# Differential attention: a score block as one product of 128 rows in place of two

## The chip, the cores and the metric

The kernel runs on one core of a Trainium2 chip. Time is device time in microseconds (us) from the start to the end of one execution of the program. Four engines work side by side and meet at semaphores: PE (TensorE, the matrix products), DVE (VectorE), ACT (ScalarE) and POOL (GpSimd, hardly used here); SP issues the DMA transfers. Each engine has its own list of instructions, whose order is fixed when the program is built. The tiles of this kernel have 128 partitions (rows) by up to 512 columns; a product contracts over the rows of both its operands.

## The reference, cut to what matters

Two layers of a decoder trunk, 512 tokens, width 1024. Each layer is a half-step SwiGLU feed-forward block, a mixer of four groups of heads (A differential attention, B causal convolution, C gated MLP, D forgetting attention), and a second feed-forward block. The change is in group A:

```python
z = hn @ w_in[l]
qa = _rms_norm(z[..., DIFF_Q0:DIFF_K0].reshape(B, S, DIFF_HEADS, 2, DIFF_QK_DIM), diff_qk_g[l, 0])
ka = _rms_norm(z[..., DIFF_K0:DIFF_V0].reshape(B, S, DIFF_HEADS, 2, DIFF_QK_DIM), diff_qk_g[l, 1])
...
s = jnp.einsum('bqhcd,bkhcd->bhcqk', qi, k).astype(jnp.float32) * scale
causal = k_pos[None, :] <= q_pos[:, None]
p = jax.nn.softmax(jnp.where(causal, s, NEG_INF), axis=-1)
a = p[:, :, 0] - lam * p[:, :, 1]
return jnp.einsum('bhqk,bkhe->bqhe', a.astype(v.dtype), v)
```

There are 4 heads, each with two score maps (c = 0, 1) of 32 channels. Queries go in blocks of 128, so block i needs (i + 1) · 128 keys.

## The kernel before, in words

**Precision.** A value that goes into a projection or a score is kept as a high part, rounded to the operand type fp32r, and a low part, the remainder. Each projection product is three PE products: high by high, low by high, high by low (`mm3`, lines L337 to L339). Weights arrive by DMA; ACT rounds each 512-column piece to the high part `wh` (L288) and DVE subtracts to get the low part `wl` (L289).

**The mixer's order.** The input projection goes by groups: b, aqk (Q and K of group A), av, dqk, dvf (Q, K, V and gates of group D), c, then the output projection wo. While these products are written out, the work of the groups that already have their inputs is mixed in by Python generators (`chain_a` to `chain_d`): a virtual clock counts up with each product, after each projection product a `tick` lets those generators go on that are due by it, and each of them names its next due time when it yields (`GA`, two units of that clock, between steps of group A). A list scheduler then fixes each engine's order; the two instructions of `softmax` on DVE and ACT are given a higher priority. What stands between two pieces of attention on PE are projection products (called fillers below), and they are what PE does while DVE and ACT work on the attention.

**Group A.** There are 16 units per layer, unit u = 4 · head + query block. A step of `attention_gen` writes out the weighting by V of the unit two before (`poA`), `stage1_a` of this unit, and the transposes of the unit before (`ptA` on PE, copied by ACT to `pT`, L1026). `stage1_a` forms the two score blocks `scA`: in `scores` two products of 128 rows each and one bf16 product of `maskb` by `identb` that adds the mask; DVE takes the negated row maximum `nmA` (L1007), ACT the exponential (L1009). DVE then takes the reciprocal `rA`, the factor `cf` (L1184) and the combination `p` of the two maps (L1185). `ptA` waits for that `p`.

**Preparation of a head.** `prep_a(hd, 0)` makes the Q operands and `prep_a(hd, 1)` the K operands of a head; those of head hd + 1 are written out in units 1 and 2 of head hd. Four PE transposes bring `zr`, in which each 32-channel group stands twice, into PSUM (`aT`). For Q, ACT makes the high part `aTh` (L1207) and, for each map, a scaled copy `aTx` (L1212), and DVE makes of both a tile `aTs` for each map (L1214): its own 64 rows hold [high; low], the other 64 rows are zero. For K, ACT makes `aTh` and DVE the remainder `aTs` (L1219). A score block is then the Q tile by the high K tile plus the Q tile by the low K tile. Among DVE's other work are the taps of group B's convolution (`cacc`, L1130) and the scaling of group D's Q and K (`dqk`, L1279).

Of the kernel before, what the change touches and what calls it, by code (L numbers as in the profile page):

```python
# [9 lines left out]
F32 = mybir.dt.float32  # L10
F32R = mybir.dt.float32r
BF16 = mybir.dt.bfloat16
I32 = mybir.dt.int32
AF = mybir.ActivationFunctionType
ALU = mybir.AluOpType
AX = mybir.AxisListType

P = 128
# [6 lines left out]
def tile_hybrid_trunk(  # L25
# [29 lines left out]
    V, A, G, T = nc.vector, nc.scalar, nc.gpsimd, nc.tensor  # L55
# [27 lines left out]
    const = ctx.enter_context(tc.tile_pool(name="const", bufs=1))  # L83
# [4 lines left out]
    small = ctx.enter_context(tc.tile_pool(name="small", bufs=2))  # L88
# [3 lines left out]
    def blk(dt=F32, name="blk"):  # L92
        return bpool.tile([P, 512], dt, tag="blk", name=name)
# [4 lines left out]
    def att(name="at"):  # L98
        return pat.tile([P, 512], F32, tag="at", name=name)
# [38 lines left out]
    def matmul(out, fp32=True, **kw):  # L138
        n = 1
        for d in out.shape[1:]:  # L140
            n *= d
        clock[0] += max(0.107, n * (4 if fp32 else 1) / 2400.0)
        return T.matmul(out, **kw)  # L143

    def transpose(**kw):
        clock[0] += 0.107
        return T.transpose(**kw)
# [12 lines left out]
    onesc = const.tile([P, P], F32, name="onesc")  # L160
    V.memset(onesc, 1.0 / 256.0)


    slot = const.tile([P, 2, 2], F32, name="slot")
    V.memset(slot, 0.0)
    for r in range(4):
        V.memset(slot[32 * r : 32 * r + 32, r // 2, 0:1], 1.0 - 2.0 * (r % 2))
        V.memset(slot[32 * r : 32 * r + 32, r // 2, 1:2], float(r % 2))
    fold = const.tile([P, P], F32, name="fold")
    V.tensor_reduce(fold[:, :32], ident.rearrange("p (g c) -> p c g", g=4), AX.X, ALU.add)  # L170
    for g in range(1, 4):
# [244 lines left out]
    for i in range(NT // 2):  # L416
        r = wpool.tile([P, 2048], F32, tag="wl", name=f"x{i}")
# [255 lines left out]
    r = rsqrt(ss0, NT, 1.0 / D, "n000", 0, False)  # L673
# [133 lines left out]
    for q in range(1, 4):  # L807
# [8 lines left out]
        ps = att(f"adaps0{q}")  # L816
# [187 lines left out]
    def softmax(sc, n, ssum, name):  # L1004
        nm = small.tile([P, 1], F32, tag="nm", name=f"nm{name}", bufs=8)
        with tc.high_priority(offset=HX):
            V.tensor_reduce(nm, sc[:, :n], AX.X, ALU.max, negate=True)  # L1007
            p = blk(name="p")
            A.activation(p[:, :n], sc[:, :n], AF.Exp, bias=nm, accum_out=ssum)  # L1009
        return p  # L1010

    def scores(pairs, i, name, fp32=True):
        n = (i + 1) * P
        sc = att(f"sc{name}")
        for e, (q, k) in enumerate(pairs):
            matmul(sc[:, :n], fp32=fp32, lhsT=q[:, i * P : (i + 1) * P], rhs=k[:, :n], start=e == 0, stop=False,
                   skip_group_check=True)
        matmul(sc[:, i * P : n], fp32=False, lhsT=identb, rhs=maskb, start=False, stop=True, skip_group_check=True)
        return sc
# [51 lines left out]
    def mixer(l, hn, before, nxt):  # L1071
# [14 lines left out]
        V.tensor_scalar(nlam, nlam, -lam_init, None, ALU.add)  # L1086
        ogs = small.tile([P, 1], F32, tag="ogs", name=f"ogs{l}")
        V.tensor_scalar(ogs, cols[:, col_at["og"] + l : col_at["og"] + l + 1], 1.0 - lam_init, None, ALU.mult)
        gA = small.tile([P, 4], F32, tag="gA", name=f"gA{l}")
        a0 = col_at["aq"] + 2 * l  # L1090
        V.tensor_scalar(gA[:, 0:1], cols[:, a0 : a0 + 1], 32 ** -0.5, None, ALU.mult)
        V.tensor_copy(gA[:, 1:2], cols[:, a0 + 1 : a0 + 2])
        V.tensor_scalar(gA[:, 2:4], slot[:, :, 1], gA[:, 0:1], None, ALU.mult)
        gD = small.tile([P, 2], F32, tag="gD", name=f"gD{l}")
        V.memset(gD, 1.0)
        d0 = col_at["dq"] + 2 * l
# [74 lines left out]
        aT = {}  # L1171

        def stage1_a(i, hd):
            n = (i + 1) * P
            s = small.tile([P, 2], F32, tag="sA", name=f"sA{l}{i}{hd}", bufs=4)
            r = small.tile([P, 2], F32, tag="rA", name=f"rA{l}{i}{hd}", bufs=6)
            pp = []
            for cc in range(2):
                q, (kh, kl) = aT[hd][0][cc], aT[hd][1]
                sc = scores(((q, kh), (q, kl)), i, f"A{l}{i}{hd}{cc}", False)  # L1180
                pp.append(softmax(sc, n, s[:, cc : cc + 1], f"A{l}{i}{hd}{cc}"))
            V.reciprocal(r, s)
            cf = small.tile([P, 1], F32, tag="cf", name=f"cf{l}{i}{hd}", bufs=4)
            V.scalar_tensor_tensor(cf, s[:, 0:1], nlam, r[:, 1:2], ALU.mult, ALU.mult)  # L1184
            V.scalar_tensor_tensor(pp[0][:, :n], pp[1][:, :n], cf, pp[0][:, :n], ALU.mult, ALU.add)  # L1185
            if hd < H - 1 and i in (1, 2):
                prep_a(hd + 1, i - 1)
            return pp[0], r[:, 0:1]
# [11 lines left out]
        def prep_a(hd, w):  # L1200


            ps = att(f"aT{l}{hd}{w}")
            for t in range(NT):
                transpose(out=ps[:, t * P : (t + 1) * P], in_=zr[t, w][:, hd * P : (hd + 1) * P], identity=ident)
            hi = blk(F32R, "aTh")
            A.activation(hi, ps, AF.Identity, scale=gA[:, w : w + 1])  # L1207
            if w == 0:
                sts = []
                for cc in range(2):  # L1210
                    x_low = blk(name="aTx")
                    A.activation(x_low, ps, AF.Identity, scale=gA[:, 2 + cc : 3 + cc])  # L1212
                    st = blk(F32R, "aTs")
                    V.scalar_tensor_tensor(st, hi.bitcast(F32), slot[:, cc, 0:1], x_low, ALU.mult, ALU.add)  # L1214
                    sts.append(st)
                aT[hd] = [sts]
            else:
                st = blk(F32R, "aTs")
                V.scalar_tensor_tensor(st, ps, gA[:, 1:2], hi.bitcast(F32), ALU.mult, ALU.subtract)  # L1219
                aT[hd].append((hi, st))  # L1220

        def chain_a():
            rsa = rsqrt(ssa, 64, 1.0 / 32.0, f"a{l}", RSA)
# [192 lines left out]
    for l in range(L):  # L1416
        gen = start(ada_gen(36 * l + 36 if l == 0 else 36 * (l + 1)), delay=1.0 if l == 0 else AD)
        hn2 = {}
        before = ffn(l, 0, hn, before, (l, 1, hn2))
        finish(gen)  # L1420
        hn3 = {}
        before = mixer(l, hn2, before, (l, 2, hn3))
        gen = start(ada_gen(36 * (l + 1) + 32), delay=AD)
        hn = {}
        before = ffn(l, 2, hn3, before, (l + 1, 0, hn) if l + 1 < L else None)
        finish(gen)
# [30 lines left out]
```

## Time and profile before

| what | value |
| --- | --- |
| median of 3 runs | 1978.57 us (1978.0 to 1978.98) |
| the profiled execution: its own time | 1977.61 us |
| its span from the first to the last instruction | 1975.7 us |
| mean granted TensorE clock in it, as a share of 2.4 GHz | 0.995 |
| PE busy | 1953.3 us, 99% of the span |
| DVE busy | 1228.0 us, 62% |
| ACT busy | 725.0 us, 37% |

A share of the span is a mean over stages that differ. The mixer of the first layer lies at about 445 to 615 us, that of the second about 970 us later. "Busy" of PE counts an instruction until its result is out, so products that overlap count once; what one product costs in a row of products is the distance from its start to the next start (called its pitch below).

### The profile page before, as it was taken

The numbers are of one execution on the slowest core, as the hardware profiler recorded it, in microseconds if no ns is written. First come the engines' busy times: TensorE is split into PE (matmuls) and PEld (weight loads), VectorE is DVE, ScalarE is ACT, GpSimd is POOL, SyncE is SP. The second block draws the span as 40 slices with busy tenths as digits, with TensorE's granted clock in tenths as the row PEclk, the third lists the DMA queues.
The fourth block names the chain that finished last, engine by engine and source line by source line (L and its number), as shares of the span: only waits on it lengthen the run. The fifth ranks groups of instructions, "written<-read, shape, count | busy, mean of one in ns | idle before, by whom it ended". The sixth has DMA issues, their size and how long they took to land.

```text
span 1975.7 us, 26197 instructions
## 1 busy us (share of the span) xinstructions
PE 1953.3 (99%) x10296; PEld 1661.3 (84%) x10296; DVE 1228.0 (62%) x2608; ACT 725.0 (37%) x1512; POOL 5.6 (0%) x18
## 2 busy tenths in 40 slices
PE   9999999999999999999999999999999999999999
PEld 7888888997889888888898888889787898888888
DVE  7776675688977776677585333347887773333332
ACT  5323223435764323222342222234377642222230
POOL 0000000000000000000000000000000000000000
PEclk9999999999999999999999999999999999999999
DMA  9675665221212466566334332322212122332311
GB/s 306 195 251 193 212 206 177 92 77 52 70 52 76 163 222 213 197 208 211 130 129 128 107 107 89 103 95 82 86 43 70 43 78 81 119 100 93 107 64 43
DMA packets 165350, 250.54 MB, mean 127 GB/s; under 512 B 6292, under 2 KB 112236, under 8 KB 165228
## 3 DMA queue, kind: packets, MB, share of 16 engines
q1 hardware_dynamic: 164640, 247.73, 38.0%
q8 instruction: 80, 1.31, 0.3%
q0 software_dynamic: 352, 1.05, 0.2%
q14 instruction: 42, 0.34, 0.1%
q10 hardware_dynamic: 236, 0.10, 0.0%
HBM read 246.76 MB, written 2.10 MB: 126 GB/s over the span
## 4 chain that ended last, share of the span: by engine, by line
PE 91%; DVE 6%; DMA 1%; issue 1%; ACT 1%; SPq 0%; DVEq 0%
PE i L337 15%; PE i L338 15%; PE i L339 15%; PE o L337 8%; PE o L338 8%; PE o L339 8%; DVE cacc L1130 1%; PE wo L337 1%; PE wo L339 1%; PE wo L338 1%; PE ia L781 1%; DMA ada<-in_ada_w_dram 1%; DVE wl L289 1%; PE scA L143 1%; PE scD L143 1%
## 5 line engine op out<-in xcount | busy, mean ns | idle before, releaser
L289 DVE TENSOR_TENSOR wl<-w,wh 128x512 fp32r<-128x512 f32 (+3 forms) x652 | 401.3, 663 | 318.8 <-ACT wh L288 318.3
L288 ACT CAST wh<-w 128x512 fp32r<-128x512 f32 (+3 forms) x652 | 352.4, 600 | 663.8 <-issue 384.2
L337 PE MATMUL i<-hnh,wh 128*128 128x512 f32 (+1 forms) x1408 | 526.5, 376 | 2.2 <-ACT hnh L630 2.2
L338 PE MATMUL i<-hnl,wh 128*128 128x512 f32 (+1 forms) x1408 | 527.2, 375 | 0.3
L339 PE MATMUL i<-hnh,wl 128*128 128x512 f32 (+1 forms) x1408 | 526.4, 375 | 0.0
L337 PEld LDWEIGHTS i<-hnh,wh 128*128 128x128 f32 x1408 | 264.1, 188 | 49.8 <-ACT hnh L630 2.6
L338 PEld LDWEIGHTS i<-hnl,wh 128*128 128x128 f32 x1408 | 264.8, 188 | 48.0 <-DVE hnl L623 0.7
L339 PEld LDWEIGHTS i<-hnh,wl 128*128 128x128 f32 x1408 | 264.7, 188 | 47.5
L337 PE MATMUL o<-acth,wh 128*128 128x512 f32 (+1 forms) x832 | 297.9, 358 | 0.2 <-DVE h L868 0.2
L338 PE MATMUL o<-actl,wh 128*128 128x512 f32 (+1 forms) x832 | 296.8, 357 | 0.0
L339 PE MATMUL o<-acth,wl 128*128 128x512 f32 (+1 forms) x832 | 296.6, 356 | 0.0
L337 PEld LDWEIGHTS o<-acth,wh 128*128 128x128 f32 x832 | 157.2, 189 | 23.1 <-DVE h L868 0.6
L339 PEld LDWEIGHTS o<-acth,wl 128*128 128x128 f32 x832 | 157.2, 189 | 22.5
L338 PEld LDWEIGHTS o<-actl,wh 128*128 128x128 f32 x832 | 157.2, 189 | 22.5
L501 DVE SCALAR_TENSOR_TENSOR acc<-ada,cond,acc 128x512 f32<-128x512 f32 x224 | 154.5, 745 | 26.6 <-DMA ada<-in_ada_w_dram 26.4
L937 DVE TENSOR_TENSOR silu<-silu,i 128x512 f32<-128x512 f32 x82 | 56.3, 687 | 158.8 <-PE i L339 158.7
L939 ACT CAST acth<-silu 128x512 fp32r<-128x512 f32 x88 | 54.4, 618 | 223.4 <-DVE silu L937 223.4
L868 DVE SCALAR_TENSOR_TENSOR h<-o,modc,h 128x512 f32<-128x512 f32 (+1 forms) x112 | 73.9, 671 | 70.5 <-PE o L339 69.9
L1130 DVE SCALAR_TENSOR_TENSOR cacc<-yp,cwc,cacc 128x512 f32<-128x512 f32 x120 | 89.5, 746 | 1.4
L941 DVE TENSOR_TENSOR actl<-silu,acth 128x512 fp32r<-128x512 f32 x88 | 60.6, 688 | 27.4 <-ACT acth L939 27.4
L630 ACT ACTIVATE hnh<-hn,modc 128x256 fp32r<-128x256 f32 x80 | 38.9, 506 | 71.8 <-DVE hn L629 71.8
L934 ACT ACTIVATE silu<-i 128x512 f32<-128x512 f32 x82 | 48.8, 596 | 31.9 <-PE i L339 31.9
(336 smaller groups left out, 2363.1 us busy)
## 6 DMA issues: line engine op xcount, KB each, us to landing
w<-in_ffn_w_in_dram SPq DMA_DIRECT2D x166, 512.0 KB
ada<-in_ada_w_dram SPq DMA_DIRECT2D x64, 1024.0 KB
w<-in_ffn_w_out_dram SPq DMA_DIRECT2D x40, 1024.0 KB
w<-in_w_in_dram SPq DMA_DIRECT2D x18, 1024.0 KB
w<-in_w_out_dram SPq DMA_DIRECT2D x8, 1024.0 KB
w<-in_ffn_w_in_dram SPq DMA_DIRECT2D x18, 256.0 KB
fpb<-in_ada_w_dram SPq DMA_DIRECT2D x16, 256.0 KB
w<-in_ffn_w_out_dram SPq DMA_DIRECT2D x8, 512.0 KB
```

What stands on the lines that cost most here:

```text
L288: A.copy(wh[:, a], r[:, a])
L289: V.tensor_tensor(wl[:, a], r[:, a], wh[:, a].bitcast(F32), ALU.subtract)
L337: T.matmul(ps, lhsT=lh, rhs=rh, start=start, stop=False)
L338: T.matmul(ps, lhsT=lh, rhs=rl, start=False, stop=False)
L339: last_t[0] = T.matmul(ps, lhsT=ll, rhs=rh, start=False, stop=stop)
L501: last_v[0] = V.scalar_tensor_tensor(acc, src, cond[:, k : k + 1], acc, ALU.mult, ALU.add)
L868: V.scalar_tensor_tensor(h[m][:, a:b], ps[:, a:b], mcol(l, j, m), h[m][:, a:b], ALU.mult, ALU.add)
L934: A.activation(gates[j], ps, AF.Silu)
L937: last_v[0] = V.tensor_tensor(s, s, ps, ALU.mult)
L939: A.copy(ah, s)
L941: V.tensor_tensor(al, s, ah.bitcast(F32), ALU.subtract)
L1130: V.scalar_tensor_tensor(acc, ysl, w, acc, ALU.mult, ALU.add)
```

## The change

In a score block, the two products with a Q tile that is half zeros become one. The Q tile of a map now holds [high; low] in its own 64 rows and a copy of the same in the other 64; the K tile of a map holds the high part in the own 64 rows and the low part in the other 64. One product over 128 rows then sums high by high, low by high, high by low and low by low.

```diff
-    slot = const.tile([P, 2, 2], F32, name="slot")
-    V.memset(slot, 0.0)
+    slot = const.tile([P, 2], F32, name="slot")
     for r in range(4):
-        V.memset(slot[32 * r : 32 * r + 32, r // 2, 0:1], 1.0 - 2.0 * (r % 2))
-        V.memset(slot[32 * r : 32 * r + 32, r // 2, 1:2], float(r % 2))
+        V.memset(slot[32 * r : 32 * r + 32, 0:1], 1.0 - 2.0 * (r % 2))
+        V.memset(slot[32 * r : 32 * r + 32, 1:2], float(r % 2))
...
-        V.tensor_scalar(gA[:, 2:4], slot[:, :, 1], gA[:, 0:1], None, ALU.mult)
+        V.tensor_tensor(gA[:, 2:3], slot[:, 1:2], gA[:, 0:1], ALU.mult)
...
-                q, (kh, kl) = aT[hd][0][cc], aT[hd][1]
-                sc = scores(((q, kh), (q, kl)), i, f"A{l}{i}{hd}{cc}", False)
+                sc = scores(((aT[hd][0][cc], aT[hd][1][cc]),), i, f"A{l}{i}{hd}{cc}", False)
...
-            hi = blk(F32R, "aTh")
-            A.activation(hi, ps, AF.Identity, scale=gA[:, w : w + 1])
+            own = (slice(0, 64), slice(64, 128))
+            st = [blk(F32R, "aTs") for _ in range(2)]
             if w == 0:
-                sts = []
+                hi = blk(F32R, "aTh")
+                A.activation(hi, ps, AF.Identity, scale=gA[:, 0:1])
+                x_low = blk(name="aTx")
+                A.activation(x_low, ps, AF.Identity, scale=gA[:, 2:3])
                 for cc in range(2):
-                    x_low = blk(name="aTx")
-                    A.activation(x_low, ps, AF.Identity, scale=gA[:, 2 + cc : 3 + cc])
-                    st = blk(F32R, "aTs")
-                    V.scalar_tensor_tensor(st, hi.bitcast(F32), slot[:, cc, 0:1], x_low, ALU.mult, ALU.add)
-                    sts.append(st)
-                aT[hd] = [sts]
+                    a, b = own[cc], own[1 - cc]
+                    V.scalar_tensor_tensor(st[cc][a], hi[a].bitcast(F32), slot[a, 0:1], x_low[a], ALU.mult, ALU.add)
+                    A.copy(st[cc][b], st[cc][a].bitcast(F32))
+                aT[hd] = [st]
             else:
-                st = blk(F32R, "aTs")
-                V.scalar_tensor_tensor(st, ps, gA[:, 1:2], hi.bitcast(F32), ALU.mult, ALU.subtract)
-                aT[hd].append((hi, st))
+                for cc in range(2):
+                    a, b = own[cc], own[1 - cc]
+                    A.activation(st[cc][a], ps[a], AF.Identity, scale=gA[a, 1:2])
+                    V.scalar_tensor_tensor(st[cc][b], ps[a], gA[a, 1:2], st[cc][a].bitcast(F32), ALU.mult, ALU.subtract)
+                aT[hd].append(st)
```

The change also moves instructions, since the virtual clock counts the products that are gone and the scheduler places the new ones. Counted over the projection products of dqk, dvf and c (96 of dqk, then 96 of dvf, then c), so many stand on PE ahead of a unit's first score product in each layer, before and after the change: unit 3: 36 and 53; unit 6: 67 and 89; unit 8: 95 and 139; unit 9: 113 and 157; unit 10: 163 and 192; unit 11: 185 and 192; unit 12: 192 and 192; unit 15: 224 and 224.

PE's order, first layer, around unit 11 (head 2, block 3, scores of 512 columns). Before, from the mask product of its second score block to the first scores of unit 12 (`scA_4647`); `ptA_4596` belongs to unit 10 and `poA_4640` to the weighting of unit 10:

```order
L143 MATMUL scA_4584<-maskb,identb 128x128
L339 MATMUL dvf_3_4396<-wh_4153,hnl 128x260
L337 MATMUL dvf_3_4396<-wh_4153,hnh 128x260
L338 MATMUL dvf_3_4396<-wl_4154,hnh 128x260
L339 MATMUL dvf_3_4396<-wh_4153,hnl 128x260
L147 MATMUL ptA_4596<-ident,p 128x128 x3
L337 MATMUL dvf_3_4396<-wh_4153,hnh 128x260
L338 MATMUL dvf_3_4396<-wl_4154,hnh 128x260
L339 MATMUL dvf_3_4396<-wh_4153,hnl 128x260
L143 MATMUL poA_4640<-va,pT 128x64 x3
L143 MATMUL scA_4647<-aTh,aTs 128x128
```

After, the same engine from the transposes that prepare head 3's K (`aT_4513`), behind the scores of unit 10, to the first scores of unit 12 (`scA_4630`); `ptA_4524` and `poA_4555` are unit 9's, `ptA_4579` and `poA_4623` unit 10's, `scA_4561` and `scA_4568` the two score blocks of unit 11:

```order
L147 MATMUL aT_4513<-ident,zr 128x128 x4
L147 MATMUL ptA_4524<-ident,p 128x128 x2
L143 MATMUL poA_4555<-va,pT 128x64 x2
L143 MATMUL scA_4561<-aTs 128x512
L143 LDWEIGHTS identb
L143 MATMUL scA_4561<-maskb,identb 128x128
L143 MATMUL scA_4568<-aTs 128x512
L143 LDWEIGHTS identb
L143 MATMUL scA_4568<-maskb,identb 128x128
L147 MATMUL ptA_4579<-ident,p 128x128 x3
L143 MATMUL poA_4623<-va,pT 128x64 x3
L143 MATMUL scA_4630<-aTs 128x128
```

The fillers have moved ahead of unit 9 and unit 10: in this piece none is left, where before 22 stood between unit 9's transposes and its weighting, 4 ahead of unit 10's transposes and 3 ahead of its weighting. All 192 of dqk and dvf stand ahead of it, and c begins behind the transposes of unit 11 in both.

DVE's order at the same place, first layer, from the combination of unit 10 to that of unit 11. Before (`cf_4527` is unit 10's, `nmA_4580` and `nmA_4588` are unit 11's maxima):

```order
L1185 SCALAR_TENSOR_TENSOR p<-p,cf_4527 128x384
L1007 TENSOR_REDUCE nmA_4580<-scA_4576 128x1
L1007 TENSOR_REDUCE nmA_4588<-scA_4584 128x1
L289 TENSOR_TENSOR wl_4607<-w_4407,wh_4606 128x512 x2
L1182 RECIPROCAL rA_4575<-sA_4574 128x2
L289 TENSOR_TENSOR wl_4607<-w_4407,wh_4606 128x512
L1184 SCALAR_TENSOR_TENSOR cf_4593<-sA_4574,nlam_3260,rA_4575 128x1
L1130 SCALAR_TENSOR_TENSOR cacc<-yp_3567,cwc,cacc 128x512
L1185 SCALAR_TENSOR_TENSOR p<-p,cf_4593 128x512
```

After (`cf_4510` is unit 10's, `nmA_4564` and `nmA_4571` are unit 11's maxima, `nmA_4633` is the first of unit 12):

```order
L1182 SCALAR_TENSOR_TENSOR p<-p,cf_4510 128x384
L1219 SCALAR_TENSOR_TENSOR aTs<-aT_4513,gA_3264,aTs 64x512
L287 TENSOR_TENSOR wl_4590<-w_4394,wh_4589 128x512
L1005 TENSOR_REDUCE nmA_4564<-scA_4561 128x1
L1005 TENSOR_REDUCE nmA_4571<-scA_4568 128x1
L287 TENSOR_TENSOR wl_4590<-w_4394,wh_4589 128x512
L1128 SCALAR_TENSOR_TENSOR cacc<-yp_3566,cwc,cacc 128x512
L1179 RECIPROCAL rA_4560<-sA_4559 128x2
L287 TENSOR_TENSOR wl_4730<-w_4599,wh_4729 128x512
L1181 SCALAR_TENSOR_TENSOR cf_4576<-sA_4559,nlam_3259,rA_4560 128x1
L1005 TENSOR_REDUCE nmA_4633<-scA_4630 128x1
L1182 SCALAR_TENSOR_TENSOR p<-p,cf_4576 128x512
```

From unit 10's first maximum to unit 11's combination, DVE now has one `aTs`, two `wl` and one maximum more (that of unit 12); ahead of unit 10's first maximum it has three `aTs` more and one `wl` less. On ACT, after the change, one cast of the first wo chunk and then the two exponentials of unit 10, half of head 3's K, three more casts of that chunk and the other half of K stand in this order ahead of unit 9's `pT`; both exponentials of unit 11 stand ahead of unit 10's `pT`, as before, but unit 12's scores are now built on PE behind the weighting that needs that `pT` with no filler between. The second layer has the same order in all of this.

## Rows read from the trace of the kernel before

**Rows 1.** The page, section 1: busy time, share of the span, instructions.

```profile
PE 1953.3 (99%) x10296; PEld 1661.3 (84%) x10296; DVE 1228.0 (62%) x2608; ACT 725.0 (37%) x1512; POOL 5.6 (0%) x18
```

**Rows 2.** Waits of PE, whole run: us in total, times, longest us.

```profile
PE poA L143 <- ACT pT L1026: 1.8, 2, 0.9
PE ptA L147 <- DVE p L1185: 1.4, 2, 0.7
```

**Rows 3.** Windows: us, then PE, PEld, DVE, ACT, POOL busy, PEclk, DMA, GB/s.

```profile
490.00:500.00 10.00, 10.00 (x81) 9.50 (x80) 9.98 (x28) 8.02 (x23) 0.00 (x0) 1.00 0.04 8
...
510.00:520.00 10.00, 8.43 (x58) 7.06 (x56) 9.58 (x27) 8.28 (x28) 0.50 (x1) 1.00 0.39 133
```

**Rows 4.** Timeline of PE, units 10 to 13: start, us, instruction, [idle before].

```profile
503.51 0.42 PE L143 MATMUL scA<-aTh,aTs 128*128 128x384 f32 x1
503.77 0.34 PE L143 MATMUL scA<-aTs 128*128 128x384 f32 x1
503.95 0.23 PE L143 MATMUL scA<-maskb,identb 128*128 128x128 bf16 x1
...
505.28 0.28 PE L339 MATMUL dvf<-wh,hnl 128*128 128x260 f32 x1
...
507.67 0.28 PE L338 MATMUL dvf<-wl,hnh 128*128 128x260 f32 x1
...
508.46 0.40 PE L143 MATMUL scA<-aTs 128*128 128x512 f32 x1
508.70 0.23 PE L143 MATMUL scA<-maskb,identb 128*128 128x128 bf16 x1
...
511.64 0.88 PE L143 MATMUL poA<-va,pT 128*128 128x64 f32 x6 [0.89 <-ACT pT L1026]
...
512.47 0.28 PE L143 MATMUL scA<-aTs 128*128 128x128 f32 x1
512.59 0.23 PE L143 MATMUL scA<-maskb,identb 128*128 128x128 bf16 x1
...
513.79 0.63 PE L147 MATMUL ptA<-ident,p 128*128 128x128 f32 x4 [0.68 <-DVE p L1185]
...
516.77 0.28 PE L143 MATMUL scA<-aTs 128*128 128x256 f32 x1
516.89 0.23 PE L143 MATMUL scA<-maskb,identb 128*128 128x128 bf16 x1
```

**Rows 5.** Timeline of DVE, from unit 10's first maximum to unit 12's.

```profile
504.22 0.56 DVE L1007 TENSOR_REDUCE nmA<-scA 128x1 f32<-128x384 f32 x1
...
507.14 0.73 DVE L1219 SCALAR_TENSOR_TENSOR aTs<-aT,gA,aTh 128x512 fp32r<-128x512 f32 x1
507.79 0.21 DVE L1184 SCALAR_TENSOR_TENSOR cf<-sA,nlam,rA 128x1 f32<-128x1 f32 x1
...
510.25 1.28 DVE L289 TENSOR_TENSOR wl<-w,wh 128x512 fp32r<-128x512 f32 x2
...
512.24 0.74 DVE L1130 SCALAR_TENSOR_TENSOR cacc<-yp,cwc,cacc 128x512 f32<-128x512 f32 x1
512.90 0.74 DVE L1185 SCALAR_TENSOR_TENSOR p<-p,cf 128x512 f32<-128x512 f32 x1
513.56 0.28 DVE L1007 TENSOR_REDUCE nmA<-scA 128x1 f32<-128x128 f32 x1
```

**Rows 6.** Instructions of the tile aTx: count, min/median/max ns, starts.

```profile
L1212 ACT ACTIVATE aTx<-aT,gA x16: 679/694/717, 453.0 to 1474.4; 128x512 f32<-128x512 f32 x16
```

**Rows 7.** Windows of PE, head 0's preparation: us, busy, PEclk, DMA, GB/s.

```profile
448.00:450.00 2.00, 0.03 (x1) 1.00 0.00 0
...
454.00:456.00 2.00, 2.00 (x7) 0.50 0.00 0
456.00:458.00 2.00, 2.00 (x6) 0.50 0.74 150
458.00:460.00 2.00, 2.00 (x15) 0.96 0.99 382
```

More of the change, by code (lines that the diff above doesn't have):

```diff
@@ L1088, in mixer @@
         V.tensor_scalar(ogs, cols[:, col_at["og"] + l : col_at["og"] + l + 1], 1.0 - lam_init, None, ALU.mult)
-        gA = small.tile([P, 4], F32, tag="gA", name=f"gA{l}")
+        gA = small.tile([P, 3], F32, tag="gA", name=f"gA{l}")
         a0 = col_at["aq"] + 2 * l
```

## The prediction, as put on record before the run

> **What bounds the kernel now.** First the page's busy times: PE is busy for 99% of the span, ACT for 37% [rows 1]. So the run is PE's own row of products, and a change counts if it shortens that row or breaks it. Second the windows of the mixer, which the average hides: from 490 to 500 us PE and DVE are both full (10.00 and 9.98 of 10 us), from 510 to 520 DVE has 9.58 and PE falls to 8.43 [rows 3]. There DVE is a second bound, just behind PE. Third PE's waits: for group A's softmax it waits 1.8 us for `pT` and 1.4 us for `p` in the whole run, twice each, so 0.9 and 0.7 us per layer [rows 2]. Fourth PE's timeline shows where: at 511.64 and at 513.79, round units 11 and 12 of layer 1 [rows 4]. During these waits products of c stood behind in PE's list, which need nothing of the attention, and PE did not take them first: an instruction that waits holds the queue. Last, DVE's timeline is an unbroken row from unit 10's first maximum at 504.22 to unit 11's combination, which ends at 512.90 + 0.74 = 513.64; PE's transposes start at 513.79, when it is done [rows 4, 5].
>
> **What the change removes.** Each unit loses the second score product of both maps. Its price is the distance from its start to the mask product's: 0.12 us at 128 columns, 0.12 at 256, 0.18 at 384, 0.24 at 512 [rows 4]. Per head 2 × (0.12 + 0.12 + 0.18 + 0.24) = 1.32 us, per layer 5.28, in the run 10.6 us of PE, all on the path where PE is full. The Trainium skill (TensorE: Matmul & The Clock Gate, Back-to-back issue gap) gives an isolated product columns/2.4 + 2.5 ns; worked out, an estimate, 8.7 us in the run. The rows are longer at small widths, 0.12 against 0.056, and they decide.
>
> **What it adds.** ACT: per head six instructions for four; I price a half-height one like a full one, 0.69 us long [rows 6], an estimate, since no row has 64 rows of 512 columns. That is 8 × 0.69 = 5.5 us per layer at most. It hides while ACT has room (8.02 and 8.28 busy of 10 us [rows 3]) but not where a `pT` stands behind it, which I count below. DVE: four `aTs` for three per head. The full-height one holds DVE for 507.79 − 507.14 = 0.65 us [rows 5]. Bounds for the half-height one: 0.33 (half the rows, half the time) and 0.65; I take 0.65, since what an instruction takes in these rows goes with columns (maxima 0.28 at 128, 0.56 at 384), and columns don't change. So +4 × 0.65 = 2.6 us per layer, in the very stretch where DVE has none to spare.
>
> **What it moves.** The order shows the larger effect. Attention now lags behind the projection: dqk and dvf run out ahead of unit 10, and units 10, 11 and 12 stand on PE with no filler between. Before, 22 + 4 + 3 fillers covered the way from unit 9's transposes to unit 10's weighting. PE will wait there for the whole chain through ACT and DVE. I follow it to one checkpoint, the start of unit 11's transposes (`ptA`, four), ahead of which all 192 products of dqk and dvf, and none of c, stand in both programs; it was at 513.79 [rows 4].
>
> 1. PE reaches unit 10's scores at 503.51 before. One filler is (507.67 − 505.28)/20 = 0.12 us [rows 4] (20 fillers from the one start to the other); 192 − 163 = 29 more ahead cost 3.5 us, and the products gone from units 0 to 9 give back two heads, 2 × 1.32, and 4 × 0.12 of units 8 and 9, 3.1 us. So 503.9: PE is no later, and has just spent its cover.
> 2. DVE ahead of unit 10's maximum: three `aTs` more, one `wl` less. A `wl` is 1.28/2 = 0.64 [rows 5]: +1.3 us. The maximum, at 504.22 before, lies between 504.4 (scores at 503.9 and the half microsecond of the product) and 505.5 (DVE's queue).
> 3. From there to the end of unit 11's `p` took 9.4 us [rows 5]. Added to DVE: one `aTs` 0.65, two `wl` 1.28, unit 12's maximum 0.28 [rows 5]: 11.6. So `p` ends between 516.0 and 517.1 if nothing else waits.
> 4. Something else does. Unit 12's maximum stands ahead of `p` on DVE, and its scores stand behind unit 10's weighting on PE, which needs unit 10's `pT`, which ACT now has behind both exponentials of unit 11. That closes a loop through three engines: bound 0 to 1.2 us, the last as long as two exponentials at 0.6 us, an estimate from ACT rows of that size [rows 6]. I take 517.4 for the end, PE at 517.5: 3.7 us behind 513.79.
>
> Behind the checkpoint, units 12 to 15 give back one head, 1.3 us. Net +2.4 us per layer at full clock; PE is the bound again behind it, so the loss is kept to the end.
>
> **The clock.** From about 504.9 (unit 10's scores and the aT transposes done) to 517.5 PE has only two small weightings, two units' scores and three transposes, some 3 us: it waits about 9 us, the longest stretch about 4 to 5 us, while ACT works off exponentials, K's preparation and three weight casts ahead of unit 9's `pT`. The trace shows what such a gap does: PE was idle from 448 to 450, and granted half the clock (0.50, so 1.2 GHz) as late as 456 to 458, full from 458 to 460 on, though it was busy all through from 454 [rows 7]. The short waits at 511 and 513 left the clock at 1.00 [rows 3]. So I expect the fall here. It costs about half of the 4 us after the restart, as at 454 to 458 [rows 7]: 2.0 us, and 0.3 on the score products inside the chain. Per layer 2.4 + 2.3 = 4.7, both layers +9.4. The Trainium skill says the same (TensorE: Matmul & The Clock Gate, What's actually happening): the clock is throttled by default and activity releases it; this trace agrees, with 0.50 behind an idle 2 us.
>
> **The sum.** 1977.61 + 9.4 = 1987.0 us for a profiled run; the median of the runs lies 0.96 above the profiled one, so 1988.
>
> **Rivals.** *Attention keeps pace* (ends on the other side). If ACT's and DVE's half-height instructions are near half the price, or the chain is not late otherwise, PE's waits stay below what they were, 1.6 us per layer [rows 2], and all 10.6 us are gained: about 1968. For it: DVE would carry 0.65 less per `p`. Against it: the chain of step 3 has 9.4 us of work that it had before, and only 2.5 us of PE work stands ahead of unit 11's transposes to cover it. It decides where the waits per layer fall below 5.3 us, the gain per layer. Chance 0.17. *The clock holds*: stalls as worked out but no fall: 1978.57 + 4.8 = 1983. Gaps of 0.9 us did hold [rows 3], 2 us did not [rows 7]; if the wait breaks into pieces, it may. Chance 0.19. *The stall eats the gain only*: PE waits some 5 us in each layer, and the time stays at 1977 to 1981; this is the chain at the lower bounds, 516.0 and without the loop, which gives 516.1 − 513.79 − 1.3 = +1.0 per layer, 1980.6. Chance 0.12. *Longer stalls*: the same lag opens gaps at units 13 to 15 as well, 8 us per layer and more: above 1995. Against it: products of c are there as cover from unit 12 on. Chance 0.06.
>
> **How the numbers follow.** The likeliest is the forecast with the fallen clock, 0.46, at 1988 (its own range 1984 to 1993). This kernel's measurement tells 0.2%, some 4 us, from no change. Slower by more, above 1982.5: 0.46, the longer stalls, and half of the case at 1983: 0.62. Within 0.2%: the other half, and most of the stall that only eats the gain: 0.20. Faster: 0.18. The range leaves out the gain in full and the longest stalls: 1974 to 1995.
>
> **What would show it.** PE's waits for `pT` (L1024 there) and for `p` (L1182) grow from 3.2 us to about 18 to 20 in the run, at 505 to 518 and some 970 us later. The product that is gone: PE's count falls by 64 score products, and scA is one product and one mask. The half-height `aTs` shows 0.6 to 0.7 us; at 0.4 the DVE part fails. The granted clock dips to 0.5 round 508 to 520, and the mean falls below 0.995. If unit 11's transposes start by 514 the chain argument is wrong, and the run is near 1968; if they start at 517 and the clock stays at 1.00, only the last term is wrong.

## The result and the profile after

The changed kernel takes 1990.72 us (median of 4 runs, 1989.37 to 1991.35) against 1978.78 us of the kernel before: a ratio of 1.0061, 95% interval 1.0049 to 1.0073. So it is slower by 12 us, where 9.4 were forecast. Its profiled run took 1989.37 us, 11.8 above that of before, with a span of 1987.6 us and a mean granted clock of 0.989 (0.995 before). One execution used below is unlike the rest: the profiled one of the run with taps on POOL took 2500.91 us at a mean granted clock of 0.739, its four others 2072.0 to 2074.96 us at 0.968, and only the lengths of single instructions and who waits for whom are read from it.

The busy times of the changed kernel's profile (to be read against [rows 1]): PE has 64 instructions less and the same busy time, ACT 16 and DVE 7 more.

```profile
PE 1953.0 (98%) x10232; PEld 1659.9 (84%) x10232; DVE 1236.7 (62%) x2615; ACT 736.8 (37%) x1528; POOL 5.6 (0%) x18
```

PE's waits of the whole run (us, times, longest). Those for `pT` were 1.8 us in two pieces [rows 2] and are now 14.7 in eight; that for `p` hardly moved.

```profile
PE poA L143 <- ACT pT L1024: 14.7, 8, 5.5
...
PE ptA L147 <- DVE p L1182: 1.6, 2, 0.8
```

The windows of layer 1 (columns as in [rows 3]). From 500 to 520 PE has 12.0 busy us of 20, and the granted clock falls to 0.50.

```profile
490.00:500.00 10.00, 9.81 (x81) 9.10 (x81) 9.25 (x21) 7.87 (x22) 0.00 (x0) 1.00 0.33 106
500.00:510.00 10.00, 6.17 (x48) 5.29 (x46) 9.94 (x29) 9.27 (x23) 0.00 (x0) 0.93 0.01 2
510.00:520.00 10.00, 5.83 (x24) 4.66 (x25) 8.67 (x20) 5.30 (x16) 0.75 (x1) 0.50 0.37 119
520.00:530.00 10.00, 10.00 (x51) 8.22 (x50) 7.57 (x21) 7.11 (x20) 0.00 (x0) 0.88 0.05 14
```

Before, PE had no idle time from 500 to 510:

```profile
500.00:510.00 10.00, 10.00 (x81) 9.13 (x80) 9.71 (x27) 6.84 (x17) 0.25 (x1) 1.00 0.28 100
```

Windows of PE alone (us, busy, clock, DMA, GB/s) show the order: PE falls idle at 506.6, the clock falls within 508 to 510 and is back only within 522 to 524.

```profile
506.00:508.00 2.00, 0.58 (x4) 1.00 0.00 0
508.00:510.00 2.00, 0.00 (x0) 0.67 0.00 0
510.00:512.00 2.00, 0.00 (x0) 0.50 0.00 0
...
520.00:522.00 2.00, 2.00 (x7) 0.50 0.15 58
522.00:524.00 2.00, 2.00 (x16) 0.92 0.00 0
```

PE's timeline, from unit 10's scores to unit 11's transposes (start, us, instruction, [idle before]):

```profile
504.91 0.42 PE L143 MATMUL scA<-aTs 128*128 128x384 f32 x1
...
506.17 0.44 PE L147 MATMUL ptA<-ident,p 128*128 128x128 f32 x2
512.06 1.12 PE L143 MATMUL poA<-va,pT 128*128 128x64 f32 x4 [5.46 <-ACT pT L1024]
...
516.48 1.54 PE L143 MATMUL poA<-va,pT 128*128 128x64 f32 x6 [1.32 <-ACT pT L1024]
...
519.50 1.09 PE L147 MATMUL ptA<-ident,p 128*128 128x128 f32 x4 [0.79 <-DVE p L1182]
```

The longest wait, 5.46 us, is for unit 9's `pT`. ACT's timeline shows what stood ahead of that copy: two exponentials of unit 10, half of head 3's K, three casts, and the other half of K, which waited for DVE's first K instruction. PE had the transposes ready at 506.6; the copy ran at 511.64.

```profile
507.04 0.58 ACT L1007 ACTIVATE p<-scA,nmA 128x384 f32<-128x384 f32 x1
...
507.61 0.58 ACT L1007 ACTIVATE p<-scA,nmA 128x384 f32<-128x384 f32 x1
...
508.16 0.68 ACT L1218 ACTIVATE aTs<-aT,gA 64x512 fp32r<-64x512 f32 x1
508.73 1.66 ACT L286 CAST wh<-w 128x512 fp32r<-128x512 f32 x3
510.93 0.68 ACT L1218 ACTIVATE aTs<-aT,gA 64x512 fp32r<-64x512 f32 x1 [0.54 <-DVE aTs L1219]
511.64 0.37 ACT L1024 COPY pT<-ptA 128x256 f32<-128x256 f32 x1
```

DVE's timeline (against [rows 5]): unit 10's first maximum at 505.72, the first of its two instructions for K at 510.15, behind two `wl` and three `dqk`, and unit 11's `p` done at 518.61 + 0.74 = 519.35. Ahead of it DVE itself stood idle for 1.11 us, for unit 12's scores.

```profile
505.72 0.55 DVE L1005 TENSOR_REDUCE nmA<-scA 128x1 f32<-128x384 f32 x1
...
510.15 0.74 DVE L1219 SCALAR_TENSOR_TENSOR aTs<-aT,gA,aTs 64x512 fp32r<-64x512 f32 x1
...
518.40 0.29 DVE L1005 TENSOR_REDUCE nmA<-scA 128x1 f32<-128x128 f32 x1 [1.11 <-PE scA L143]
518.61 0.74 DVE L1182 SCALAR_TENSOR_TENSOR p<-p,cf 128x512 f32<-128x512 f32 x1
```

DVE alone, from the first zr transpose of layer 1 (the first product that prepares head 0) to the end of unit 11's `p`, before and after (us, busy, clock, DMA, GB/s). DVE is busy for 5.0 us more on this way and idle for 1.6 us more; the way is 6.6 us longer. In layer 2 it is the same 5.0 and 1.6.

```profile
450.09:513.64 63.55, 55.71 (x131) 0.95 0.17 55
449.17:519.35 70.18, 60.74 (x137) 0.88 0.18 59
```

Instructions of the tile `aTs` (count, min/median/max ns): half the rows take the whole time (before, 128x512 took 746 and 743 on DVE, and 694 on ACT [rows 6]).

```profile
L1212 DVE SCALAR_TENSOR_TENSOR aTs<-aTh,slot,aTx x16: 705/748/753, 454.3 to 1483.1; 64x512 fp32r<-64x512 f32 x16
L1218 ACT ACTIVATE aTs<-aT,gA x16: 674/682/685, 454.4 to 1489.9; 64x512 fp32r<-64x512 f32 x16
L1213 ACT CAST aTs<-aTs x16: 617/618/619, 455.1 to 1484.1; 64x512 fp32r<-64x512 f32 x16
L1219 DVE SCALAR_TENSOR_TENSOR aTs<-aT,gA,aTs x16: 743/751/757, 455.8 to 1491.3; 64x512 fp32r<-64x512 f32 x16
```

**A measure that holds still.** The profiled runs differ by some us before the mixer is reached, though PE has the same products up to there (the first zr transpose starts at 449.2 to 455.8 us in the profiles of this table; the clock of the first 40 us differs, from 0.81 to 0.99 in windows of 20 us). So the mixer is measured by itself, on PE's timeline: from the start of the first zr transpose to the first product of the next feed-forward block behind the last one of wo (its length), and to the first transpose of unit 15's `p` (its attention). Layer 1 / layer 2, in us:

| kernel | unit 15 | mixer's length |
| --- | --- | --- |
| before | 82.9 / 83.4 | 182.1 / 182.8 |
| changed | 90.1 / 90.9 | 189.5 / 190.3 |
| new preparation, two products | 91.9 / 93.8 | 192.6 / 194.4 |
| old preparation, one product | 83.5 / 84.8 | 182.0 / 183.3 |
| changed, K's ACT instructions first | 89.8 / 91.0 | 188.7 / 190.2 |
| the same, Q copies on POOL | 89.7 / 89.3 | 188.2 / 187.8 |
| changed, dummy products | 87.1 / 86.2 | 186.3 / 185.5 |
| old preparation, one product, dummies | 82.7 / 85.4 | 182.0 / 184.7 |
| changed, c ahead of dvf | 87.6 / 88.0 | 219.2 / 219.7 |

The mixers of the changed kernel are 7.4 and 7.5 us longer; the 11.8 us of the whole profiled run are 3.1 less than their sum, which the stretches outside the mixers gave back (0.9 ahead of the first, about 1 in each of two others). Why those got shorter was not looked into.

### The profile page after: what moved, and what is told of

It is laid out like the page before. It is cut to its first block, busy times and chain, and to the rows that moved or that the text cites. A ratio compares the mean times of both kernels' runs of the same rounds, so it can differ in the third digit from the quotient of the medians.

```text
span 1987.6 us, 26084 instructions
## 1 busy us (share of the span) xinstructions
PE 1953.0 (98%) x10232; PEld 1659.9 (84%) x10232; DVE 1236.7 (62%) x2615; ACT 736.8 (37%) x1528; POOL 5.6 (0%) x18
## 4 chain that ended last, share of the span: by engine, by line
PE 90%; DVE 6%; ACT 2%; issue 1%; DMA 1%; SPq 0%; DVEq 0%; ACTq 0%
PE i L335 15%; PE i L336 15%; PE i L337 15%; PE o L335 8%; PE o L336 8%; PE o L337 8%; DVE cacc L1128 2%; PE wo L336 1%; PE wo L337 1%; PE wo L335 1%; PE poA L143 1%; PE scD L143 1%; PE poD L143 1%; PE b L337 1%; PE b L336 1%
## 5 line engine op out<-in xcount | busy, mean ns | idle before, releaser
L335 PEld LDWEIGHTS o<-acth,wh 128*128 128x128 f32 x832 | 157.2, 189 | 22.7 <-DVE h L866 0.2
L935 DVE TENSOR_TENSOR silu<-silu,i 128x512 f32<-128x512 f32 x82 | 56.3, 687 | 158.4 <-PE i L337 158.3
```

The costliest lines, as they stand in the source:

```text
L335: T.matmul(ps, lhsT=lh, rhs=rh, start=start, stop=False)
L935: last_v[0] = V.tensor_tensor(s, s, ps, ALU.mult)
```

## The experiments

**The two halves of the change apart.** New preparation with both products:

```diff
-                sc = scores(((aT[hd][0][cc], aT[hd][1][cc]),), i, f"A{l}{i}{hd}{cc}", False)
+                sc = scores(((aT[hd][0][cc], aT[hd][1][cc]), (None, aT[hd][1][cc])), i, f"A{l}{i}{hd}{cc}", False)
```

For `None`, `scores` takes a tile of zeros, `zq`, as the stationary operand.

> The new preparation with the old number of score products: each score block has a second product again, with a zero tile as its stationary operand, so it adds nothing. If the new preparation (its longer way through ACT and DVE) makes the stalls of units 9 to 12, they stay, and the 10.6 us of products come back on top of the changed kernel's 1990.7, less what falls into the stalls: 1996 to 2001. If the stalls come from the missing products, which covered the softmax, PE's waits go back to about 3 us in the run and the time is that of the kernel before, 1977 to 1981.

Measured: 2002.24 us (1999.25 to 2003.31), ratio 1.0113, 1.0098 to 1.0128, 1.2 us above the upper end of what the first reason expected. Its waits:

```profile
PE poA L143 <- ACT pT L1026: 12.1, 8, 4.3
```

The stalls are there with all products in place. So it does not take the missing products to make them: the new preparation, with the order that the scheduler gives it, is enough (143 projection products of dqk and dvf stand ahead of unit 9 here, 113 before, and 180 and 163 ahead of unit 10). Its mixers are 10.5 and 11.6 us longer than before, 3.1 and 4.1 us longer than those of the changed kernel: behind the new preparation the second products do cost time.

Old preparation with one product:

```diff
-                sc = scores(((q, kh), (q, kl)), i, f"A{l}{i}{hd}{cc}", False)
+                sc = scores(((q, kh),), i, f"A{l}{i}{hd}{cc}", False)
```

> The kernel before with the second score product (Q by low K) left out and its old preparation: the scores lack the low part of K. If the new preparation makes the stalls: the removed products are gained nearly whole, 1967 to 1971, with waits of PE for pT and p below 6 us in the run. If the missing products make them (the order shows dqk and dvf used up ahead of unit 11 here too): no gain, 1976 to 1985.

Measured: 1978.67 us (10 runs, 1975.7 to 1985.06), ratio 0.9997, 0.9986 to 1.0008: nothing is gained, as the second reason expected. The removed time went into waits for `pT` and a fall of the clock (the view of waits, then windows with the columns as above):

```profile
PE poA L143 <- ACT pT L1026: 6.6, 4, 1.9
```

```profile
500.00:510.00 10.00, 7.79 (x62) 6.85 (x61) 9.54 (x24) 7.90 (x20) 0.76 (x1) 1.00 0.15 58
510.00:520.00 10.00, 8.75 (x41) 7.50 (x41) 8.31 (x25) 5.69 (x22) 0.00 (x0) 0.66 0.43 131
```

Counted from the first zr transpose, unit 11's transposes come at 63.1 and 61.9 us (63.7 and 64.2 before): up to there 0.6 and 2.3 us are gained, of some 4 us of products that are gone. At unit 15 nothing is left of it (83.5 and 84.8): around these units the clock was at a half, from 510 to 517 in layer 1 and for 13.7 us in layer 2. What holds unit 11 is DVE, whose row has hardly a gap from 485 to 515, before (first line) and here (columns as in the windows of DVE above):

```profile
485.00:515.00 30.00, 29.16 (x73) 1.00 0.18 57
485.00:515.00 30.00, 28.61 (x71) 0.92 0.19 54
```

So the attention, by DVE's row, and not PE's row of products alone, already set the pace of this stretch in the kernel before; its 0.9 and 0.7 us of waits [rows 2] fit that. This is read from the rows; no run makes DVE's row shorter and leaves the order of the rest as it was.

**What of the preparation?** K's two ACT instructions ahead of its two DVE instructions:

```diff
                 for cc in range(2):
+                    a = own[cc]
+                    A.activation(st[cc][a], ps[a], AF.Identity, scale=gA[a, 1:2])
+                for cc in range(2):
                     a, b = own[cc], own[1 - cc]
-                    A.activation(st[cc][a], ps[a], AF.Identity, scale=gA[a, 1:2])
                     V.scalar_tensor_tensor(st[cc][b], ps[a], gA[a, 1:2], st[cc][a].bitcast(F32), ALU.mult, ALU.subtract)
```

> The changed kernel with K prepared as two ACT instructions and then two DVE instructions, not ACT, DVE, ACT, DVE. If ACT's second K instruction, which waits there for DVE's first and holds up unit 9's pT, is the cause: the longest wait of PE falls from 5.5 us by about half a microsecond to 2 us and the run to 1985 to 1989. If the sheer number of instructions on ACT and DVE is the cause: 1989 to 1992.

Measured: 1991.71 us (1990.3 to 1995.14), ratio 1.0066, 1.0049 to 1.0083: as the changed kernel. The longest wait fell from 5.5 to 3.4 us, as expected, but the time did not follow; unit 15 is where it was.

```profile
PE poA L143 <- ACT pT L1024: 12.4, 8, 3.4
```

And with it the Q copies on POOL:

```diff
-                    A.copy(st[cc][b], st[cc][a].bitcast(F32))
+                    nc.gpsimd.tensor_copy(st[cc][b], st[cc][a].bitcast(F32))
```

> As the run before, and the two Q copies of each head on POOL in place of ACT, which then has four preparing instructions per head as before the change. If ACT's queue (copies, K, casts ahead of pT) makes the stall: PE's waits for pT fall below 8 us in the run and the time to 1974 to 1984. If DVE's extra half-height instructions make it: still 1986 to 1991. If POOL's copies take much longer than the 0.62 us of ACT, the scores of each next head come late instead: above 1990.

Measured: 1991.25 us (1989.29 to 1992.26), ratio 1.0059, 1.0044 to 1.0074. ACT has no more preparing instructions than before the change, and unit 9's transposes come almost as early as in the kernel before (56.3 and 55.1 us after the first zr transpose; 54.9 and 55.3), but unit 11's again 4.5 and 2.6 us later (68.2 and 66.8; 63.7 and 64.2; 70.3 and 70.9 in the changed kernel). PE still waits 13.2 us for `pT`. So the ping-pong and ACT's copies are not the whole cause. How much of it they are this run does not say: while POOL copies, 11 DVE instructions get longer, by 4.2 us in the run (on this effect see below), and of the 2.1 and 4.1 us won at unit 11 only 0.4 and 1.6 are left at unit 15, with the clock at a half from 509 to 523 in layer 1.

**The clock.** Dummy products ahead of two weightings, where PE waited. In the kernel with the old preparation and one product, 24 ahead of unit 9's and 32 ahead of unit 10's:

```diff
         po = att(f"po{name}")
+        if name[0] == "A" and hd == 2 and i in (1, 2):
+            for _ in range(24 if i == 1 else 32):
+                T.matmul(po[:, :64], lhsT=identb, rhs=maskb[:, :64], start=True, stop=True, skip_group_check=True)
```

> The kernel before with the second score product left out (as in the run that gave 1978.7), and dummy products into the output block of the next weighting where PE waited: 24 ahead of unit 9's weighting, 32 ahead of unit 10's, overwritten by the real ones. The scores lack the low part of K. If the granted clock of 0.50 from 510 to 517 took most of what the removed products gave: the clock stays at 1.00 there and the run falls to 1970 to 1975. If the waits themselves took it: 1977 to 1981.

Measured: 1981.29 us (10 runs, 1979.25 to 1988.02), ratio 1.001, 1.0001 to 1.002. The clock stayed at 1.00 to 516 and then fell all the same (0.50 from 518 to 520), with four waits of 0.3 to 1.0 us from 513 to 518. It was at a half for 3.4 and 10.2 us in the two layers, for 6.8 and 13.7 without the dummies, and the mixers are no shorter, 182.0 and 184.7. So the hope for the clock was a miss, and the second reason fits, 0.3 us above its range: unit 11 comes at 62.4 and 62.1 us, hardly other than without dummies (63.1 and 61.9), at the full clock up to there.

In the changed kernel, with 64 and 24 of them (the same lines):

> The changed kernel with 64 dummy products ahead of unit 9's weighting and 24 ahead of unit 10's. The scheduler also puts unit 11's first score block ahead of unit 9's weighting. If the clock is a separate term of the loss: granted clock 1.00 from 505 to 523 and 2 to 4 us less per layer, 1982 to 1987. If the waits alone are the loss: 1989 to 1993, at whatever clock.

Measured: 1986.86 us (6 runs, 1984.67 to 1990.97), ratio 1.0038, 1.0026 to 1.005; the mixers are 3.2 and 4.8 us shorter than in the changed kernel. Windows of PE:

```profile
512.00:514.00 2.00, 1.03 (x25) 1.00 0.00 0
514.00:516.00 2.00, 1.08 (x5) 0.76 0.00 0
516.00:518.00 2.00, 2.00 (x23) 0.50 0.09 18
518.00:520.00 2.00, 1.99 (x22) 0.88 0.39 129
```

In layer 1 the clock is at a half for 3.4 us in place of 13 to 14. In layer 2 it stays at 1.00 from 1480 to 1510; the middle one of three windows:

```profile
1490.00:1500.00 10.00, 7.39 (x66) 1.00 0.38 127
```

There the mixer takes 185.5 us: 4.8 of the 7.5 us by which the changed kernel's was longer are gone, and 2.7 are left at the full clock. That and the time agree with a clock term of the expected size, but unit 11's first score block also stands ahead of unit 9's weighting here, and the run does not part the two.

**DVE's load.** The last 16 taps of the second half of B's convolution on POOL:

```diff
...
+                            nc.gpsimd.tensor_scalar(pt1, y[:, tap : tap + S], w, None, ALU.mult)
+                            nc.gpsimd.tensor_tensor(pacc, pacc, pt1, ALU.add)
...
```

> The changed kernel with the last 16 taps of the second half of group B's convolution taken from DVE and given to POOL (two instructions each), some 16 times 0.66 us less on DVE per layer. If DVE's queue sets the pace of units 8 to 12: PE's waits for pT and p fall below 8 us in the run and the time to 1972 to 1983. If it is the length of the way through ACT and DVE and not the load: 1988 to 1992. If POOL is much slower than 1 us per instruction, the mean over the convolution comes late and PE waits for it: above 1992.

Measured: 2074.34 us, ratio 1.0477, 1.0459 to 1.0494. This is the third case of the expectation: a tap on POOL takes 1.65 + 1.28 us against 0.75 on DVE, so POOL needs some 44 us for 15 of them, and the sum comes late. DVE waits for it in its queue with the attention behind. The run says nothing of DVE's load. Groups of POOL:

```profile
L1129 POOL TENSOR_SCALAR ptap<-yp,cwc 128x512 f32<-128x512 f32 x30 | 49.6, 1652 | 2.0 <-issue 2.0
L1130 POOL TENSOR_TENSOR pacc<-pacc,ptap 128x512 f32<-128x512 f32 x30 | 38.4, 1279 | 0.2
```

Two of four `wl` subtractions of each mixer chunk on POOL, in the changed kernel, in the one before, and in the one with one product and the old preparation:

```diff
-        V.tensor_tensor(wl[:, a], r[:, a], wh[:, a].bitcast(F32), ALU.subtract)
+        e = nc.gpsimd if n in mixset and q in (1, 3) else V
+        e.tensor_tensor(wl[:, a], r[:, a], wh[:, a].bitcast(F32), ALU.subtract)
```

> The changed kernel with two of the four low-part subtractions of each mixer weight chunk on POOL in place of DVE, 8 of the 16 that stand on DVE between the first maxima of units 0 and 15. If DVE's queue sets the pace of group A: 8 times 0.64 us less on it, the mixer (first zr transpose to the first product of the next feed-forward block, 189.5 us before this edit) gets 3 to 7 us shorter in each layer, 1977 to 1985 in all. If A's way goes through ACT and the waits between engines and not DVE's load: 1988 to 1992. If POOL's subtraction, which takes longer, brings the weights late: above 1992, with PE waiting for wl.

> The kernel before with the same subtractions on POOL. If the kernel before is bound by PE in its mixer as the 99% say: within 2 us of 1979, since DVE has room on average. If A's chain through DVE bounds the mixer already: up to 5 us less per layer, 1968 to 1976.

> The kernel before without the second score product (the scores lack the low part of K) and with the same subtractions on POOL. If removed PE work gave nothing because A's chain through DVE set the length of the mixer, and DVE is now relieved: 1966 to 1974, and 3 us or more below the run before this one. If DVE's load is not what holds the chain: 1977 to 1980 as without POOL.

Measured: 2023.09, 2006.0 and 2015.95 us; ratios 1.0223 (1.0205 to 1.024), 1.0138 (1.0112 to 1.0164) and 1.0182 (1.0166 to 1.0197). All three are slower, against both theories. The time of the first fits its third case, but its sign does not: PE waits for `pT`, `zr` and `sacc`, which hang on DVE's row, and not for `wl`. What the rows show is on DVE itself: while POOL subtracts (1.40 us each), single DVE instructions get longer. The convolution's taps, first in the kernel before, then with the subtractions on POOL (count, min/median/max ns):

```profile
L1130 DVE SCALAR_TENSOR_TENSOR cacc<-yp,cwc,cacc x120: 728/746/753, 418.4 to 1511.9; 128x512 f32<-128x512 f32 x120
```

```profile
L1134 DVE SCALAR_TENSOR_TENSOR cacc<-yp,cwc,cacc x120: 723/751/1885, 423.3 to 1528.3; 128x512 f32<-128x512 f32 x120
```

In the kernel before with the subtractions on POOL, 130 DVE instructions overlap one of the 60 subtractions. Together they take 41 us more than the same groups took in the kernel before (medians), and all others no more; the 60 subtractions would have been 60 × 0.64 = 38 us on DVE. So these runs did not relieve DVE and don't decide. Why a balance of 3 us on DVE costs 26 us is not parted: the order changed too. The last run takes work from DVE without POOL:

```diff
-                for tap in range(TAPS):
+                for tap in range(TAPS - (30 if m else 0)):
...
```

> The changed kernel without 30 of the 31 taps of the second half of group B's convolution (that half is left out of the result), so 30 times 0.66 us less on DVE per layer, half of it between the scores of units 5 and 12, and nothing on POOL. If DVE's queue sets the pace of group A: dqk and dvf last to unit 12, the transposes of unit 15 start 78 to 84 us after the first zr transpose as in the kernel before (82.9; 90.1 in the changed kernel), the clock stays at 1.00 from 490 to 530, and the run takes 1966 to 1978. If the way through ACT and the ping-pong in the preparation set it: unit 15 stays at 87 to 91 us and the run at 1986 to 1991.

Measured: 2003.08 us (2000.86 to 2006.43), ratio 1.0119, 1.0101 to 1.0136; unit 15 at 95.7 and 94.6. DVE is busy for 6.91 us of 10 from 500 to 510 and PE waits 15.4 us for `pT` in the run. The window (columns as above):

```profile
500.00:510.00 10.00, 4.64 (x24) 4.21 (x23) 6.91 (x16) 7.41 (x19) 0.00 (x0) 0.63 0.30 107
```

With the taps gone, group B's closing steps came forward into the attention of heads 1 and 2: six ACT instructions of theirs, one of them 0.84 us late for DVE, and two exponentials stand ahead of unit 7's `pT`, for which PE waits 5.36 us. So this run is no clean test, neither of the preparation nor of DVE's load: DVE has room, but the order changed with it. It shows that room on DVE alone doesn't bring the attention forward: what stands ahead of `pT` on ACT can hold it as well.

**Cover.** The projection of c ahead of dvf:

```diff
-    ORDER = ('b', 'aqk', 'av', 'dqk', 'dvf', 'c')
+    ORDER = ('b', 'aqk', 'av', 'dqk', 'c', 'dvf')
```

> The changed kernel with the projection of group C ahead of that of D's V, so that 11 to 51 fillers stand in each of the units 9 to 15 of group A. If missing cover makes the stalls there: PE's waits for pT and p of group A fall below 5 us in the run and the clock stays at 1.00 there. The last two heads of group D then have no filler: their waits take its place, 1.5 to 3 us for each of 8 units, 24 to 48 us in the run less what A gives back: 1990 to 2020 in all. If A's waits come from its own way through ACT and DVE whatever stands between, they stay above 12 us.

Measured: 2052.36 us (2052.19 to 2053.18), ratio 1.0366, 1.0351 to 1.0382. As the first reason expected, A's waits fell below 5 us and those of D took their place; but the time is 32 us above its range, for more: PE also waits 17.2 us for the inputs of C's gating product. Waits:

```profile
PE poD L143 <- ACT pT L1024: 17.1, 16, 1.5
...
PE poA L143 <- ACT pT L1024: 3.6, 8, 0.8
```

The clock is at 1.00 from 480 to 540. That agrees with missing cover as what makes A's stalls and the fall of the clock there. How long the attention's own way is, this run does not show. Unit 15 comes at 87.6 and 88.0 us, but 273 projection products stand ahead of its scores, 224 before, and 96 of them are c's with 512 columns, 32 before. PE's own row is that long: up to these scores of layer 1 it is busy as follows, before and here (columns as in the windows of PE).

```profile
450.09:526.87 76.78, 73.55 (x453) 0.96 0.22 73
451.58:534.40 82.82, 81.41 (x468) 0.96 0.16 49
```

## Why the prediction was right, and where it was not

- **Direction and size.** Forecast 1988, range 1974 to 1995; measured 1990.7. The place was right too: PE's waits came at units 9 to 12 of both layers, behind fillers that had run out, for `pT` more than for `p`. That the number is so near is in part luck: the two mixers lost 14.9 us where 9.4 were forecast, and some 3 us came back outside them, which no step has.
- **What the change removes.** The step said that the 10.6 us lie on the path "where PE is full". Alone they give nothing (ratio 0.9997). In the kernel before, the attention's row on DVE was as long as the products that cover it: 29.16 us busy of 30. The rows of DVE at 9.98 of 10 us and the short waits [rows 2, 3] pointed to it, and the text itself called DVE a second bound, just behind PE; the sum then took the products as a gain of PE and only afterwards followed DVE.
- **What it adds.** The price of a half-height instruction as that of a full one is confirmed: 0.75 us long on DVE, 0.62 to 0.68 on ACT. Half the rows save nothing. What one holds DVE for, to the next start, was put at 0.65; the sixteen of the first layer hold it for 0.74 each, the twelve before for 0.68.
- **The order.** The text on the change gave two reasons for the lag of the attention, the virtual clock and the scheduler. The first is wrong: with one line more, so that the virtual clock counts the removed products too, the program that is built has the same order on every engine. The lag in the order is the scheduler's, which places the new preparation and the shorter row of products.
- **The four steps to the checkpoint.** Step 1 had PE at unit 10's scores at 503.9; it was 504.91, although the mixer began 0.9 us earlier. The step took PE's row up to there to be without new gaps; PE was idle for 2.0 us from the first zr transpose to these scores, 1.1 before, 0.42 of it for unit 8's `pT`. The rest of the 1.9 us is not placed. (The attention lagged in heads 0 and 1 too: unit 2's transposes come 22.7 us after the first zr transpose, 19.6 before.) Step 2 gave 504.4 to 505.5 for the maximum: 505.72. Step 3 gave 11.6 us from there to `p`, step 4 up to 1.2 more: it took 13.6, of which 1.11 are the forecast wait for unit 12's scores. The checkpoint came at 519.50 and not at 517.5. That is the mis-sized term: 5.7 us late (6.6 counted from the first zr transpose) in place of 3.7. Steps 2 and 3 add 3.5 us to DVE's row up to there; it is 5.0 us longer, 3.7 of it by four more `aTs` (16 × 0.74 for 12 × 0.68 us, where 4 × 0.65 were counted) and 0.8 by one more `wl`.
- **Behind the checkpoint** 1.3 us should have come back from units 12 to 15. From unit 11 to unit 15 it took 19.2 us before and 19.8 after: the clock was at a half until 522, and that fits a loss larger than what the products gave.
- **The clock.** It fell as forecast, to 0.50, and was back some 10 us after PE resumed at 512, not 4; PE waited twice more in between. PE was busy at a half for 1.94 + 1.15 + 1.52 + 1.21 + 2.00 us from 512 to 522 in windows of 2 us, 7.8 us, so some 3.9 us of lost speed against the 2.3 forecast, a part of it inside waits that would have been there anyway.
- **The sum of it.** Idle time of PE from 500 to 520 rose from 1.6 us, all of it behind 510 [rows 3], to 8.0; with about 3.9 for the clock and 5.3 of products less that is 5.0 of the 7.4 us in layer 1. The other 2.4 are not placed by these rows. These are terms of one sum and overlap in part, so they are an estimate.
- **The rivals.** Attention keeps pace: no, the waits for `pT` and `p` are 16.3 us in the run (18 to 20 were forecast), some 8 per layer and above the 5.3 from which it decides. The clock holds: no.
- **Still open.** What of the longer way is due to the added instructions themselves and what to the new order. The rows put 5.0 of the 6.6 us to unit 11 on DVE's own row, but no run tests that: those that were to relieve DVE made its instructions longer (POOL) or changed the order (fewer taps). The ACT to DVE ping-pong alone is not it, since it could be taken away without a gain; the Q copies on ACT are not the whole of it. No run holds the order of the kernel before fixed. No version here beats the kernel before; the best with the change, with dummy products, is 0.38% slower.

## What to carry to other kernels

An engine that is busy for 99% of the span need not be the one that sets the pace: where its few waits fall together with another engine that is full (here DVE, 29.16 of 30 us), the two are of one length, and work taken from the first comes back as waits. Count what a smaller product costs in preparation on the other engines, by instructions and not by rows, and look at what stands ahead of the copy that the first engine will wait for. Before trusting an edit to the gain in products, run the removal alone: here it would have shown at once that this removal by itself wins nothing.

## What was not expected of the hardware

- A POOL instruction lengthens what DVE does at the same time: taps of 0.75 us took up to 1.88 us, and moving 60 subtractions of the run from DVE to POOL made the kernel before 26 us slower (1.38%). The 20 row maxima among the 130 that overlap, with one input, from PSUM, did not get longer. The Trainium skill (SBUF — State Buffer, Who interferes with whom, and Summary: rules for kernel authors) says that of a DVE instruction with two SBUF inputs and a GpSimd instruction that reads SBUF the one that issues second blocks until the first has finished; a tap has two such inputs, and its longest time agrees with a tap and most of a POOL instruction of 1.40 us in a row.
- A granted clock at a half outlasts its cause. An idle stretch of 5.46 us ended at 512.06, the clock stayed at 0.50 until 522, with waits of 1.32 and 0.79 us on the way; in the kernel before, waits of 0.89 and 0.68 us [rows 4] met a full clock and left it there [rows 3].
- Two runs with the same PE products up to the mixer differ with the clock of their first 40 us: 0.81 and 0.84 in the two 20 us windows there (one product with dummies) against 0.95 and 0.97 (the kernel before) went with a mixer that began 5.7 us later.
